# Fourier layer of a two-layer diffusion block: adding and subtracting mirrored tokens ahead of the input projection

## Chip, cores and metric

The kernel runs on one core of one Trainium2 chip. The metric is the device time of one execution in microseconds (us); lower is better.

## What is computed

Two layers run over 2048 latent tokens of 1024 channels in float32. Layer 0 is attention. Layer 1, which the change touches, mixes by a two-dimensional Fourier transform: over the positions, and over the 256 channels of each of four groups. Cut to what matters:

```python
def fourier_layer(x, shift, scale, gate, norm_g, w_in, w_out):
    h = modulate(x, norm_g, shift, scale)
    u, g = jnp.split(h @ w_in, 2, axis=-1)
    uf = u.reshape(b, n, F_GROUPS, F_GROUP_DIM).astype(jnp.float32)
    f = jnp.fft.fft2(uf, axes=(1, 3), norm="ortho").real.astype(x.dtype).reshape(b, n, F_WIDTH)
    return x + gate * ((f * jax.nn.silu(g)) @ w_out)
```

The real part of the transform of u needs, of every channel group, a cosine transform over the channels (even in the position's sign) and a sine transform (odd in it). So only sums of tokens n and N-n meet the cosine part, and only differences meet the sine part.

## The kernel before

Every float32 product is made of three matmuls in a rounded one-pass type: `split` (lines 43 to 51) writes an operand as a high and a low part, `mm3` (lines 54 to 57) multiplies high by high, high by low and low by high. The phases are 1 (input projection of layer 0), 2 (attention, in a hand-written order), 3a (its output projection, and the modulated norm of layer 1 written to DRAM as `h2`, lines 768 to 826), 3b (Fourier input projection), 3c (transform over positions, lines 972 to 1045) and 3d (output projection and final norm). Outside phase 2 a planner orders each engine's instructions by its own estimate of when they are ready; the chip then runs each engine's queue in that order.

At the start, `startup` (line 203) multiplies the left half of the layer's weights by the channel transform, so that 3b projects straight into transformed channels; 32 pieces of 128x256 are evacuated by ScalarE and stored to DRAM as `wur` by ScalarE's DMA queue (lines 236 and 237), cosine and sine columns of a group in one store.

The tokens lie in four blocks of 512: n, N/2-n, N/2+n and N-n. Phase 3b (line 941) runs twice, first over the blocks n and N-n, then over N/2-n and N/2+n. Each run goes through four sets of 512 columns: cosine (`ci` 0), sine (1), and two sets of the gate (2, 3). For each set `load_w4` loads and splits the weights into tiles `whi`, `wlo` of two rows of tiles each (five buffers), with GpSimd for the high and VectorE for the low part. For each block `load_h2` loads `h2` once, in eight pieces `hraw` of 128x512 (four buffers), and splits them into `ghi`, `glo`. Each of the four 128-token tiles of a block takes 24 matmuls of 512 columns for each set. Of sets 0 and 1 the first block's result is copied to `z`; the second's meets it on VectorE, which folds n with N-n (`fold_first`) and then N/2-n with N/2+n onto the first fold (`fold_second`), and ends with the operands EH, EL, OH, OL and the second ones E1, O1. Of the gate's sets the result goes through Silu and is stored as `g2`. `nyq` and N1, NH, NL carry the middle channel of each group; `quarter` carries the tokens N/4 and 3N/4, which have no partner.

All loads named here go through SP's DMA queue (`ld`), all stores through ScalarE's (`st`); each queue issues in order. SBUF is handed out from two sides, and pools that follow each other reuse the same bytes: a tile waits for the last reader of what lay there. Phase 3c loads its 12 tables `ch`, `cl`, `sh`, `sl` through GpSimd's queue, for three sets of positions (258, 256 and 512 columns), into bytes that phase 3b used; its matmuls are as in 3b, with 258, 256 and 512 columns.

Of the kernel before, what the change touches and what calls it, by code (L numbers as in the profile page):

```python
# [35 lines left out]
NDFT = 1026  # L36
TOKEN_GROUPS = (0, 3, 1, 2)     # blocks of tokens in the order that folding takes them

# input projection columns
# [47 lines left out]
def block_kernel(ctx: ExitStack, tc: tile.TileContext, a):  # L87
# [23 lines left out]
    wur_d = [dt_(f"wur{i}", [P, D]) for i in range(8)]  # L111
# [3 lines left out]
    # ---------------------------------------------------------------- constants  # L115
# [16 lines left out]
    # lambda on every partition, negated  # L132
# [12 lines left out]
    # bounded where the reference's norm is zero anyway; an infinite lambda still gives NaN  # L145
# [4 lines left out]
    # the score scale goes with the query gain (a power of two for the other heads)  # L150
# [30 lines left out]
    def rstd(ss, n, inv):  # L181
        """1 / sqrt(ss * inv + eps), one Newton step on the table's root."""
# [20 lines left out]
    def startup(pool, grp, pp, cb):  # L203
        """Modulations of layer 0, and W_u times the real channel transform for every group."""
        rc = pool.tile([P, 2, 256], F32, name="rc")
# [7 lines left out]
        for g in range(4):  # L213
            for b in range(2):
# [15 lines left out]
                for dt in range(4 * b, 4 * b + 4):  # L230
                    ps = pp.tile([P, 512], F32, name="wur", tag="mm", bufs=5)
                    for k in range(2):
                        T.matmul(ps[:, 0:256], u[k][:, (dt % 4) * P:(dt % 4 + 1) * P], rc[:, k, :],
                                 start=k == 0, stop=k == 1)
                    o = pool.tile([P, 256], F32, name="wuo", tag="wuo", bufs=4)
                    S.copy(o, ps[:, 0:256])
                    st(wur_d[dt].rearrange("p (s c) -> p s c", s=2)[:, :, g * P:(g + 1) * P],
                       o.rearrange("p (s c) -> p s c", s=2))
# [3 lines left out]
    # ------------------------------------------------- phase 1: input projection  # L242
    with ExitStack() as ph:
# [51 lines left out]
        def rope(src, cos, sin, nh, dim):  # L295
            """src * cos + swap(src) * sin, the halves of each axis swapped."""
# [28 lines left out]
        def put_T(src, dsts, t, stack=False):  # L325
# [4 lines left out]
            if stack:  # L330
                # rows of each half: 64 rounded, then 64 of what rounding left
# [12 lines left out]
        def evac(kind, ps, t, rp):  # L344
            """ps: 128 tokens x 512 columns of the projection; t: key tile."""
# [25 lines left out]
        # modulations of layer 1 and both gates, a tile at a time  # L371
# [61 lines left out]
    class Factors:  # L433
        """Of the differential heads' rows, s1 * o each, at the tokens of groups g0 to g1:
        1 / sqrt(mean(o^2) + eps), and zero where the reference's sum of squares leaves float32."""
# [4 lines left out]
        def steps(self, pool):  # L440
            """One instruction at a time."""
# [28 lines left out]
    # ------------------------------------------------------- phase 2: attention  # L470
    with ExitStack() as ph:
# [7 lines left out]
        KP = L // 3                                   # columns of a key or value piece  # L479
        QT = 256                                      # queries of a pair of tiles  # L480
# [3 lines left out]
        def load_split(pool, src, name, eng=(None, None)):  # L484
            """Thirds of a [128, L] scratch array as hi and lo."""
# [18 lines left out]
        def load_q(rows, tag, eng=(None, None)):  # L504
            """rows: DRAM row sets stacked on partitions."""
# [8 lines left out]
        class Task:  # L514
            """Scores of 128 queries against all keys, and exp(s - max) with its row sum."""
# [4 lines left out]
            def S(self, i):  # L520
                """Scores of segment i, which the task before has left."""
# [13 lines left out]
            def M(self, i):  # L535
                """Maximum of a segment."""
# [8 lines left out]
            def E(self, i):  # L545
                """exp of a segment."""
# [7 lines left out]
            def X(self):  # L554
                """Row sum; the first of a combination is ready with it."""
# [15 lines left out]
            def Z(self):  # L571
                """Subtracts the second probabilities, times lambda and in units of the first's sum."""
# [6 lines left out]
            def tail(self, op, i):  # L579
                """The same of the very last, in parts and on two engines."""  # L580
# [14 lines left out]
        class Pair:  # L595
            """o^T of 256 queries from two probability tiles."""
# [4 lines left out]
            def F(self):  # L601
                """Rows of a pair that is through."""
# [4 lines left out]
            def Q(self):  # L607
                """Their squares, and over the channels the sums of these."""
# [11 lines left out]
        class Item:  # L620
            """Two key tiles of a pair: transposes, split, V^T P^T."""
# [54 lines left out]
        def begin(n):  # L676
            """Pairs, tasks and items of a step: 256 queries of a head, and what they need."""
# [72 lines left out]
    def out_proj(pp, lp, us, wg, x, add):  # L750
        """x += gate * u^T w for the tokens i of x's four tiles; yields each i when done."""
# [16 lines left out]
    with ExitStack() as ph:  # L768
# [9 lines left out]
        def second_mod(x, t):  # L778
            """Modulated norm of x for layer 1, transposed."""
# [48 lines left out]
    # --------------------------- phase 3b: Fourier input projection, token folding  # L828
    with ExitStack() as ph:
        dp = ph.enter_context(ExitStack())  # L830
        sp = dp.enter_context(tc.tile_pool(name="eo", bufs=1, reuse_waits="tile"))
        # tokens n and N/2 - n folded onto n < N/4: sums (even positions) as hi and lo, and
        # differences (odd positions)
        EH, EL, OH, OL = [sp.tile([P, 4, 512], F32R, name=nm) for nm in ("EH", "EL", "OH", "OL")]
# [4 lines left out]
        with ExitStack() as pb:  # L839
# [54 lines left out]
            def fold_second(ci, j, z, ps):  # L894
                """Tokens N/2 - n (z) and N/2 + n (ps): the second fold."""
                if j == 0:
                    quarter(ci, ps)
# [312 lines left out]
```

## Time and profile before

| | |
|---|---|
| time, median of 3 runs | 2800.76 us (2798.21 to 2805.19) |
| span of the profiled execution, first to last instruction | 2799.0 us |
| mean granted clock of TensorE, share of full speed | 0.979 |
| TensorE busy with matmuls | 2675.6 us, 96% of the span |
| VectorE, ScalarE, GpSimd busy | 1762.1, 1395.5, 1201.1 us |
| phase 3b on TensorE | about 2193 to 2548 us |
| phase 3c on TensorE | about 2548 to 2598 us |

The profile gives no time of the profiled execution beyond its span; the span lies 1.8 us below the median of the runs and inside their range. Matmuls are pipelined: the profile gives one of 512 columns some 0.39 us, but the next one starts 0.23 us later, so what a matmul costs is read from the distance of starts. A line such as L55 to L57 is that of the helper `mm3`, so groups are told apart by their tiles; the moving operand stands first (`mm<-whi,ghi` has the weights moving over stationary tokens: sets 0 and 1; `mm<-ghi,whi` is the gate).

### The profile page before, as it was taken

How to read it: one execution, taken by the hardware profiler on the slowest of the kernel's cores; microseconds unless marked ns; L12 is line 12 of the kernel's file. 1: busy time of each engine (PE TensorE's matmuls, PEld its weight loads, DVE VectorE, ACT ScalarE, POOL GpSimd, SP SyncE). 2: the span in 40 equal slices, each digit the busy share in tenths (PEclk: the TensorE clock that was granted, in tenths of full speed). 3: DMA queues.
4: the chain of work that ended last, by engine and by line, in shares of the span. 5: the costliest groups of instructions: out<-in, count | busy, mean ns of one | idle time of the engine just before them, and what ended most of it. 6: DMA issues, size and time to landing. Idle time of an engine off the chain costs nothing.

```text
span 2799.0 us, 44286 instructions
## 1 busy us (share of the span) xinstructions
PE 2675.6 (96%) x15452; PEld 2322.7 (83%) x15452; DVE 1762.1 (63%) x3817; ACT 1395.5 (50%) x3700; POOL 1201.1 (43%) x1120
## 2 busy tenths in 40 slices
PE   4999998999989999999999999999899899999898
PEld 3788887887869999999989999998788688888687
DVE  7653635655248888888878888888663312322754
ACT  3631214312148888788878888888353302111312
POOL 3131421324157667766876777765322111011400
PEclk7999999999999999999999999999999999999999
DMA  9356354463410002000300011002683523128342
GB/s 325 114 140 181 93 164 160 108 188 97 147 66 20 18 20 71 18 20 20 97 23 20 20 46 31 20 19 76 215 273 132 176 75 133 48 76 226 119 153 91
DMA packets 217775, 282.51 MB, mean 101 GB/s; under 512 B 19184, under 2 KB 130496, under 8 KB 217552
## 3 DMA queue, kind: packets, MB, share of 16 engines
q1 hardware_dynamic: 115984, 197.84, 22.1%
q10 hardware_dynamic: 95232, 73.43, 8.4%
q0 software_dynamic: 6336, 8.41, 1.3%
q8 instruction: 123, 2.02, 0.3%
q14 instruction: 100, 0.82, 0.1%
HBM read 197.74 MB, written 81.83 MB: 100 GB/s over the span
## 4 chain that ended last, share of the span: by engine, by line
PE 70%; DVE 3%; POOL 1%; DMA 1%; issue 1%; ACT 1%; SPq 0%; DVEq 0%; ACTq 0%; POOLq 0%
PE s L531 16%; PE mm L57 9%; PE mm L55 9%; PE mm L56 9%; PE ptr L631 9%; PE pv L55 5%; PE pv L57 5%; PE pv L56 5%; DVE m L539 1%; PE tr L785 1%; POOL e L593 0%; PE s L615 0%; DMA u<-uy 0%; DVE tl L639 0%; PE pa L55 0%
## 5 line engine op out<-in xcount | busy, mean ns | idle before, releaser
L539 DVE TENSOR_REDUCE m<-s 128x1 f32<-128x512 f32 (+1 forms) x960 | 579.0, 632 | 174.0 <-PE s L531 169.1
L551 ACT ACTIVATE e<-s,nm 128x512 f32<-128x512 f32 (+1 forms) x960 | 614.2, 653 | 51.3 <-DVE nm L543 47.9
L635 ACT CAST th<-ptr 128x512 fp32r<-128x512 f32 x576 | 340.3, 591 | 145.6 <-PE ptr L631 130.6
L639 DVE TENSOR_TENSOR tl<-ptr,th 128x512 fp32r<-128x512 f32 x576 | 379.3, 681 | 38.3 <-ACT th L635 38.2
L57 PE MATMUL mm<-whi,glo 128*128 128x512 f32 x944 | 372.5, 396 | 3.9 <-DVE glo L51 3.9
L55 PE MATMUL mm<-whi,ghi 128*128 128x512 f32 x944 | 370.4, 396 | 1.8 <-DVE ghi L50 1.8
L56 PE MATMUL mm<-wlo,ghi 128*128 128x512 f32 x944 | 371.6, 395 | 0.0
L631 PE MATMUL ptr<-ident,e 128*128 128x128 f32 x2304 | 349.5, 274 | 20.2 <-DVE tl L639 11.4
L593 POOL TENSOR_TENSOR e<-e 128x768 f32<-128x768 f32 x189 | 342.7, 1844 | 0.0
L48 POOL TENSOR_SCALAR whi<-wraw 128x1024 fp32r<-128x1024 f32 x88 | 106.3, 1211 | 523.0 <-PE mm L56 200.3
L631 PEld LDWEIGHTS ptr<-ident,e 128*128 128x128 f32 x2304 | 271.9, 141 | 48.2 <-POOL e L593 7.2
L531 PE MATMUL s<-kB,qh 128*128 128x512 f32 (+1 forms) x768 | 285.0, 380 | 6.8 <-ACT e L551 6.8
L590 POOL TENSOR_SCALAR e<-e,rs 128x768 f32<-128x768 f32 x192 | 170.6, 912 | 220.2 <-DVE rs L566 220.2
L531 PE MATMUL s<-kB,ql 128*128 128x512 f32 (+1 forms) x768 | 252.0, 341 | 0.0
L51 DVE TENSOR_TENSOR wlo<-wraw,whi 128x1024 fp32r<-128x1024 f32 x88 | 114.1, 1299 | 181.8 <-POOL whi L48 181.7
L308 POOL TENSOR_TENSOR t<-qn,rope 128x256 f32<-128x256 f32 (+1 forms) x128 | 116.2, 929 | 252.2 <-issue 102.9
L57 PEld LDWEIGHTS mm<-whi,glo 128*128 128x128 f32 x944 | 178.2, 189 | 42.5 <-DVE glo L51 5.5
L55 PEld LDWEIGHTS mm<-whi,ghi 128*128 128x128 f32 x944 | 178.5, 189 | 39.4 <-issue 2.0
L56 PEld LDWEIGHTS mm<-wlo,ghi 128*128 128x128 f32 x944 | 178.3, 189 | 36.7
L551 ACT ACTIVATION_READ_ACCUMULATOR e<-s,nm 128x1 f32 x960 | 201.7, 210 | 0.0
L55 PE MATMUL mm<-ghi,whi 128*128 128x512 f32 x512 | 199.7, 391 | 0.0
L56 PE MATMUL mm<-glo,whi 128*128 128x512 f32 x512 | 197.9, 389 | 0.0
(280 smaller groups left out, 6164.2 us busy)
## 6 DMA issues: line engine op xcount, KB each, us to landing
wraw<-in_w_in SPq DMA_DIRECT2D x56, 512.0 KB, 3.9
aw<-in_adaT SPq DMA_DIRECT2D x64, 256.0 KB, 3.0
g<-sg ACTq DMA_DIRECT2D x64, 256.0 KB, 2.5
gl<-g SPq DMA_DIRECT2D x64, 256.0 KB, 5.8
kB<-kB SPq DMA_DIRECT2D x24, 384.0 KB, 3.8
awr<-in_adaT SPq DMA_DIRECT2D x32, 256.0 KB, 4.9
xt<-in_x SPq DMA_DIRECT2D x16, 512.0 KB, 4.4
ql<-qB SPq DMA_DIRECT2D x128, 64.0 KB, 2.2
```

Of the source, the lines that this page charges most:

```text
L55: nc.tensor.matmul(out, lh, rh, start=start, stop=False)
L56: nc.tensor.matmul(out, lh, rl, start=False, stop=False)
L57: nc.tensor.matmul(out, ll, rh, start=False, stop=stop)
L308: Q.tensor_tensor(out=o5[:, :, :, b, :], in0=s5[:, :, :, 1 - b, :], in1=sn[:, :, b, :].unsqueeze(1).to_broadcast([P, nh, 2, q]), op=ALU.mult)
L531: T.matmul(ps[:, c - o:c - o + cw], l, r[c // KP][:, k:k + cw], start=(j == 0), stop=(j == len(self.terms) - 1))
L539: V.tensor_reduce(out=self.m3[:, i:i + 1], in_=self.segs[i][:, 0:SEG[i][1]], axis=AX.X, op=ALU.max)
L551: S.activation(self.e[:, o:o + w], self.segs[i][:, 0:w], AF.Exp, bias=self.nm, accum_out=self.s3[:, i:i + 1])
L590: eng.tensor_scalar(out=self.e[:, sg], in0=self.e[:, sg], scalar1=by, scalar2=1.0, op0=ALU.mult, op1=ALU.mult)
L593: eng.tensor_tensor(out=onto[:, sg], in0=onto[:, sg], in1=self.e[:, sg], op=ALU.add)
L631: T.transpose(self.tr[:, k, i, :], self.p.es[i][:, kt * P:(kt + 1) * P], ident)
L635: S.copy(self.th, self.tr.rearrange("p k i q -> p k (i q)"))
L639: V.tensor_tensor(out=self.tl, in0=self.tr.rearrange("p k i q -> p k (i q)"), in1=self.th.bitcast(F32), op=ALU.subtract)
```

## The change

Mirrored blocks of `h2` are added or subtracted before the projection instead of after it. A fold (`load_fold`) loads the pieces of both blocks of a pair, adds or subtracts them on VectorE, sets the token without a partner with one or two GpSimd instructions on a single column, and splits the result. `project` sends sums through the cosine columns alone and differences through the sine columns alone. The gate's sets move into `gates`, which loads `h2` by itself. The order is now: gate of the first pair, sums and differences of the first pair, differences and sums of the second, gate of the second pair. The operands share one ring of 20 tiles (high and low part of one 128x512 piece each).

The middle channel gets a column of its own among the cosines, so that there are 4 x 129 = 516 of them, done as two matmuls of 258 columns; `wur` grows to 1028 columns and is stored by two DMAs for each piece instead of one. Token N/4 of the sums goes through a projection of its own, one row wide. Nothing else of phases 1 to 3a and 3d changes; 3c takes the middle channel from EH, EL.

```diff
-                    st(wur_d[dt].rearrange("p (s c) -> p s c", s=2)[:, :, g * P:(g + 1) * P],
-                       o.rearrange("p (s c) -> p s c", s=2))
+                    st(wur_d[dt][:, g * 129:(g + 1) * 129], o[:, 0:129])
+                    st(wur_d[dt][:, CW + g * P:CW + (g + 1) * P], o[:, 129:257])
...
+            def operand(src):
+                t = hp.tile([P, 2, G], F32R, name="hl", tag="hl", bufs=20)
+                split(nc, t[:, 0, :], t[:, 1, :], src, S)
+                return t[:, 0, :], t[:, 1, :]
+            def load_raw(g, kt):
+                raw = wk.tile([P, G], F32, name="hraw", tag="hraw", bufs=4)
+                ld(raw, h2_d[:, kt, g * G:(g + 1) * G])
+                return raw
+            def load_fold(half, op):
+                out = []
+                for kt in range(KT):
+                    a_, b_ = [load_raw(g, kt) for g in TOKEN_GROUPS[2 * half:2 * half + 2]]
+                    e = wk.tile([P, G], F32, name="hf", tag="hf", bufs=2)
+                    V.tensor_tensor(out=e, in0=a_, in1=b_, op=op)
+                    if op is ALU.add or half == 0:
+                        Q.tensor_copy(e[:, 0:1], a_[:, 0:1])
+                        if half == 0 and op is ALU.add:
+                            Q.tensor_copy(h34[:, kt:kt + 1], b_[:, 0:1])
+                    else:
+                        Q.tensor_tensor(out=e[:, 0:1], in0=b_[:, 0:1], in1=h34[:, kt:kt + 1], op=ALU.subtract)
+                        Q.tensor_tensor(out=h4[:, kt:kt + 1], in0=b_[:, 0:1], in1=h34[:, kt:kt + 1], op=ALU.add)
+                    out.append(operand(e))
+                return out
...
+            def project(ci, half, hs):
+                whi, wlo = load_w4(ci)
+                cols = ((0, 258), (258, 258)) if ci == 0 else ((0, 512),)
+                one, hi_, lo_ = ((E1, EH, EL), (O1, OH, OL))[ci]
+                for j in range(4):
+                    ms = slice(j * P, (j + 1) * P)
+                    for c, w in cols:
+                        ps = pp.tile([P, 512], F32, name="mm", tag="mm", bufs=5)
+                        cs = slice(c, c + w)
+                        for kt in range(KT):
+                            mm3(nc, ps[:, 0:w], hs[kt][0][:, ms], hs[kt][1][:, ms], whi[kt][:, cs], wlo[kt][:, cs],
+                                kt == 0, kt == KT - 1)
+                        e1 = one[:, j, cs]
+                        if half == 0:
+                            S.copy(e1, ps[:, 0:w])
+                            continue
...
+                        V.tensor_tensor(out=e, in0=e1, in1=ps[:, 0:w], op=(ALU.add, ALU.subtract)[ci])
+                        V.tensor_tensor(out=e1, in0=e1, in1=ps[:, 0:w], op=(ALU.subtract, ALU.add)[ci])
+                        split(nc, hi_[:, j, cs], lo_[:, j, cs], e, S)
+                if half == 1 and ci == 0:
+                    for c, w in cols:
+                        for kt in range(KT):
+                            mm3(nc, ps[0:1, 0:w], h4h[:, kt:kt + 1], h4l[:, kt:kt + 1],
+                                whi[kt][:, c:c + w], wlo[kt][:, c:c + w], kt == 0, kt == KT - 1)
...
+            gates(0)
+            project(0, 0, load_fold(0, ALU.add))
+            project(1, 0, load_fold(0, ALU.subtract))
+            odd_ = load_fold(1, ALU.subtract)
+            split(nc, h4h, h4l, h4)
+            project(1, 1, odd_)
+            project(0, 1, load_fold(1, ALU.add))
+            gates(1)
```

## Rows read from the trace of the kernel before

**Rows 1.** Page: span, and each engine's busy time, share and instructions.
```profile
span 2799.0 us, 44286 instructions
PE 2675.6 (96%) x15452; PEld 2322.7 (83%) x15452; DVE 1762.1 (63%) x3817; ACT 1395.5 (50%) x3700; POOL 1201.1 (43%) x1120
```
**Rows 2.** Page: chain of work that ended last, share by engine.
```profile
PE 70%; DVE 3%; POOL 1%; DMA 1%; issue 1%; ACT 1%; SPq 0%; DVEq 0%; ACTq 0%; POOLq 0%
```
**Rows 3.** Windows, phase 3b, its early loads, early 3c; its first row names columns.
```profile
core 0: us, PE busy (x) PEld busy (x) DVE busy (x) ACT busy (x) POOL busy (x), PEclk, DMA share, GB/s
2193.00:2549.00 356.00, 356.00 (x1556) 291.55 (x1555) 92.66 (x152) 54.02 (x94) 44.50 (x39) 0.99 0.32 100
2206.00:2214.00 8.00, 8.00 (x37) 6.63 (x36) 4.79 (x8) 5.19 (x9) 0.00 (x0) 1.00 0.77 254
2548.00:2574.00 26.00, 26.00 (x219) 25.01 (x218) 15.58 (x43) 4.86 (x9) 2.22 (x3) 1.00 0.84 246
```
**Rows 4.** Groups by form, phase 3b, TensorE: one set-0/1 group, one gate group.
```profile
L57 PE MATMUL mm<-whi,glo 128*128 128x512 f32 x256 | 100.7, 395 | 0.0
L55 PE MATMUL mm<-ghi,whi 128*128 128x512 f32 x256 | 100.0, 392 | 0.0
```
**Rows 5.** Timeline of TensorE, 512 columns, first and last of 33 consecutive starts.
```profile
2204.64 0.39 PE L57 MATMUL mm<-whi,glo 128*128 128x512 f32 x1
...
2211.90 0.39 PE L56 MATMUL mm<-wlo,ghi 128*128 128x512 f32 x1
```
**Rows 6.** Timeline of TensorE, 258 and 256 columns: start, and first start behind 216.
```profile
2548.25 0.28 PE L55 MATMUL pn<-ch,NH 128*4 128x258 f32 x1
...
2573.89 0.40 PE L55 MATMUL pn<-ch,NH 128*4 128x512 f32 x1
```
**Rows 7.** Groups by form, 2550 to 2574 us: weight loads of those matmuls.
```profile
L56 PEld LDWEIGHTS pb<-sl,OH 128*128 128x128 f32 x32 | 6.0, 188 | 0.0
```
**Rows 8.** DMA view, 2206 to 2214 us: loads, count, KB each, us to landing.
```profile
hraw<-h SPq DMA_DIRECT2D x8, 256.0 KB, 3.5
```
**Rows 9.** Waits of SP's queue, phase 3b: us in total, times, longest.
```profile
SPq L867 <- DVE wlo L51: 112.8, 14, 34.8
```
**Rows 10.** Groups by form, phase 3b, VectorE, ScalarE and GpSimd: busy, mean ns.
```profile
L51 DVE TENSOR_TENSOR wlo<-wraw,whi 128x1024 fp32r<-128x1024 f32 x30 | 37.5, 1251 | 106.5 <-POOL whi L48 106.5
L51 DVE TENSOR_TENSOR glo<-hraw,ghi 128x512 fp32r<-128x512 f32 x30 | 20.5, 716 | 24.5 <-ACT ghi L46 24.3
L915 DVE TENSOR_TENSOR e<-E,e 128x512 f32<-128x512 f32 x4 | 2.8, 692 | 0.1
L46 ACT CAST ghi<-hraw 128x512 fp32r<-128x512 f32 x27 | 16.1, 621 | 19.2 <-DMA hraw<-h 18.5 <-ACT h L789 0.4
L48 POOL TENSOR_SCALAR whi<-wraw 128x1024 fp32r<-128x1024 f32 x30 | 38.4, 1283 | 283.6 <-PE mm L56 100.4 <-DVE e L915 67.2 <-PE mm L57 67.0
```
**Rows 11.** Groups by form, 2598 to 2645 us, GpSimd busy 34 of 47 us.
```profile
L1077 DVE TENSOR_TENSOR u<-FL,gl 128x512 f32<-128x512 f32 x6 | 8.1, 1348 | 0.1
```
**Rows 12.** Instructions of one line, start-up: ns min/median/max, first and last start.
```profile
L237 ACTq DMA_DIRECT2D wur<-wuo x32: 520/521/654, 17.9 to 93.5; - x32
```
**Rows 13.** Timeline of GpSimd, phase 3c's table loads: first of each stretch, and last.
```profile
2527.06 0.96 POOL L997 DMA_DIRECT2D ch<-in_dft_ch  x1 [19.98 <-ACT sg L959]
...
2554.92 0.74 POOL L997 DMA_DIRECT2D cl<-in_dft_cl  x1 [19.23 <-DVE eL L51]
...
2556.38 0.76 POOL L997 DMA_DIRECT2D sl<-in_dft_sl  x1
```
**Rows 14.** DMA view, 2525 to 2575 us: last table load of two sets, us to landing.
```profile
sl<-in_dft_sl POOLq DMA_DIRECT2D x1, 1024.0 KB, 15.1
sl<-in_dft_sl POOLq DMA_DIRECT2D x1, 512.0 KB, 18.3
```
**Rows 15.** Timeline of TensorE, end of phase 3a.
```profile
2191.79 1.94 PE L785 MATMUL tr<-ident,xn 128*128 128x128 f32 x8 [11.74 <-DVE xn L201]
```

More of the change, by code (lines that the diff above doesn't have):

```diff
@@ L110, in block_kernel @@
     x1_d = [dt_(f"x1{i}", [P, D]) for i in range(NT)]
-    wur_d = [dt_(f"wur{i}", [P, D]) for i in range(8)]
+    wur_d = [dt_(f"wur{i}", [P, CW + 512]) for i in range(8)]
     s1_d = [dt_(f"s1r{g}", [4 * NG, P]) for g in range(NG)]
@@ L841, in block_kernel @@
             wp = pb.enter_context(tc.tile_pool(name="p4w", bufs=2, reuse_waits="tile", side="right"))
[L842 to L843 removed]
+            hp = pb.enter_context(tc.tile_pool(name="p4g", bufs=1, reuse_waits="tile", side="right"))
             wk = pb.enter_context(tc.tile_pool(name="p4k", bufs=3, reuse_waits="tile"))
[L845 removed]
@@ L846, in block_kernel @@
-            fold = pb.enter_context(tc.tile_pool(name="p4f", bufs=1, reuse_waits="tile"))
+            zp = pb.enter_context(tc.tile_pool(name="p4z", bufs=1, reuse_waits="tile"))
+            h34 = zp.tile([P, KT], F32, name="h34")
+            h4 = zp.tile([P, KT], F32, name="h4")
+            h4h, h4l = [zp.tile([P, KT], F32R, name=nm) for nm in ("h4h", "h4l")]
+            def operand(src):
+                t = hp.tile([P, 2, G], F32R, name="hl", tag="hl", bufs=20)
+                split(nc, t[:, 0, :], t[:, 1, :], src, S)
+                return t[:, 0, :], t[:, 1, :]
@@ L848, in load_h2 @@
+            def load_raw(g, kt):
+                raw = wk.tile([P, G], F32, name="hraw", tag="hraw", bufs=4)
+                ld(raw, h2_d[:, kt, g * G:(g + 1) * G])
+                return raw
             def load_h2(g):
-                grp = g0p if g < 2 else g1p
-                hi = grp.tile([P, KT, G], F32R, name="ghi", tag="ghi")
-                lo = grp.tile([P, KT, G], F32R, name="glo", tag="glo")
+                return [operand(load_raw(g, kt)) for kt in range(KT)]
+            def load_fold(half, op):
+                out = []
@@ L852, in load_h2 @@
                 for kt in range(KT):
-                    raw = wk.tile([P, G], F32, name="hraw", tag="hraw", bufs=4)
-                    ld(raw, h2_d[:, kt, g * G:(g + 1) * G])
-                    split(nc, hi[:, kt, :], lo[:, kt, :], raw, S)
-                return hi, lo
+                    a_, b_ = [load_raw(g, kt) for g in TOKEN_GROUPS[2 * half:2 * half + 2]]
+                    e = wk.tile([P, G], F32, name="hf", tag="hf", bufs=2)
+                    V.tensor_tensor(out=e, in0=a_, in1=b_, op=op)
@@ L941, in block_kernel, with quarter @@
-            for half in range(2):
+            def quarter(row, dst, n, w, blocks):
+                tr = pp.tile([P, 512], F32, name="qtr", tag="qtr", bufs=2)
+                for i, (c, cw) in enumerate(blocks):
+                    T.matmul(tr[0:cw, i:i + 1], row[0:1, c:c + cw], ones[0:1, 0:1], start=True, stop=True)
+                V.tensor_copy(dst, tr[0:n, 0:w])
+            def project(ci, half, hs):
[14 more added lines that the diff above has]
+                            continue
+                        if ci == 1 and j == 0:
+                            row = zp.tile([1, CW + 4], F32, name="row", tag="row")[:, 0:512]
+                            V.tensor_copy(row, ps[0:1, :])
+                            quarter(row, O4, P, 4, [(g * P, P) for g in range(4)])
+                        e = wk.tile([P, 512], F32, name="e", tag="ee", bufs=2)[:, 0:w]
+                        V.tensor_tensor(out=e, in0=e1, in1=ps[:, 0:w], op=(ALU.add, ALU.subtract)[ci])
+                        V.tensor_tensor(out=e1, in0=e1, in1=ps[:, 0:w], op=(ALU.subtract, ALU.add)[ci])
+                        split(nc, hi_[:, j, cs], lo_[:, j, cs], e, S)
+                if half == 1 and ci == 0:
+                    row = zp.tile([1, CW + 4], F32, name="row", tag="row")
+                    for c, w in cols:
+                        ps = pp.tile([P, 512], F32, name="mm", tag="mm", bufs=5)
+                        for kt in range(KT):
+                            mm3(nc, ps[0:1, 0:w], h4h[:, kt:kt + 1], h4l[:, kt:kt + 1],
+                                whi[kt][:, c:c + w], wlo[kt][:, c:c + w], kt == 0, kt == KT - 1)
+                        V.tensor_copy(row[:, c:c + w], ps[0:1, 0:w])
+                    V.tensor_copy(row[:, CW:CW + 4], row[:, 128:CW:129])
+                    quarter(row, E4[:, 0:4], P, 4, [(g * 129, P) for g in range(4)])
+                    quarter(row, E4[0:4, 4:5], 4, 1, [(CW, 4)])
@@ L942, in block_kernel, with gates @@
+            def gates(half):
                 groups = TOKEN_GROUPS[2 * half:2 * half + 2]
                 gh = {}
-                for ci in range(4):
+                for ci in (2, 3):
                     whi, wlo = load_w4(ci)
-                    zt = {}
                     for g in groups:
@@ L1155, in _rmat @@
     c, s = np.cos(ang) / 16.0, np.sin(ang) / 16.0
-    s[:, 0] = np.where(d[:, 0] % 2 == 0, 1.0, -1.0) / 16.0
-    return np.concatenate([c, s], 1).astype(np.float32)
+    s[:, 0] = 0.0
+    middle = np.where(d % 2 == 0, 1.0, -1.0) / 16.0
+    return np.concatenate([c, middle, s], 1).astype(np.float32)
 def _frow_perm():
```

117 lines of the change are left out of this document (23 added, 94 removed).

## Prediction, made before the changed kernel was run

> **What bounds the kernel now.** I read the page first: TensorE is busy for 2675.6 of 2799.0 us, the next engine for 63% [rows 1], and TensorE holds 70% of the chain that ended last [rows 2]. That is an average over phases, so the phase of the change is read by itself. In the window of 3b, 2193 to 2549 us, TensorE is busy for all 356 us at a granted clock of 0.99, while VectorE works 93, ScalarE 54 and GpSimd 45 us, and the DMA engines are busy for 0.32 of the time [rows 3]. So a matmul that disappears there shortens the kernel by the distance of its start to the next one, as long as the operands of what remains arrive in time. Whether they do is the question of this change: it multiplies a phase's loading and vector work and squeezes the middle of it.
>
> **TensorE's part.** Sets 0 and 1 have three groups of 256 matmuls of 512 columns, 768 in all; the gate has as many [rows 4]. Their starts are (2211.90 - 2204.64)/32 = 0.2269 us apart [rows 5]; 1536 of them make 348.5 us, which is the window but for its slow first microseconds. The change leaves 16 row tiles instead of 32 (four calls of `project`, four tiles each). The two sine calls have 2 x 4 x 24 = 192 matmuls of 512 columns, 43.6 us. The two cosine calls have 384 of 258 columns. Phase 3c has this shape: 216 matmuls of 258 and 256 columns between 2548.25 and 2573.89 us, 0.1187 us each [rows 6], with a full weight load ahead of nearly each one. So 384 cost 45.6 us. The one-row projection of token N/4 adds 48 matmuls of 258 columns with one stationary column; the nearest row has four such columns and starts at the same pace [rows 6], so 5.7 us. Removed 174.3, added 94.9: a gain of 79.4 us, all on the path. The tiny matmuls of `quarter` replace as many transposes and are taken at nothing.
>
> **Supply of the four calls.** A fold loads 16 pieces of 256 KB, a weight set 8 more: 24 for a call that lasts 22 or 23 us on TensorE (28 for the last). Before, a pair's pieces were loaded once for 174 us of matmuls. Eight `hraw` loads in the window from 2206 to 2214 us ran at 254 GB/s, with the engines at 0.77 [rows 3, 8]: 1.03 us a load, 24.8 us a call. Against that stands a lead. The ring has 20 tiles; the gate of the first pair holds 16, four are free from the start, and eight come free when its first block is done with, a quarter of the gate (22 us) before its end. So 12 of the 32 folded tiles can be there when the first call starts. The other 20, with three weight sets, are 40 + 24 = 64 loads, 16.8 MB or 66 us at that rate, and TensorE gives about 66 us before it needs the last of them. Nothing is left over, but nothing is short. VectorE needs 8 x (0.692 + 0.716) for a fold and 4 x 1.251 for the weights, 16.3 us a call, and 8.3 (four tiles by three operations at 0.692) to some 10 us more in the two calls of the second pair [rows 10]: 26 us against 22 to 28, again with the lead to draw on. ScalarE's casts (8 x 0.621) and GpSimd's (4 x 1.283) are short. The trace has no GpSimd instruction on a single column; 48 are added, in a chain VectorE, GpSimd, ScalarE, VectorE for each piece. At VectorE's price of a full piece, 0.692, they would be 33 us over four calls, under GpSimd's idle time; what they delay is the piece behind them, and four raw buffers, two pairs, cover one such delay. For the whole supply the lower bound is 0 (a gain is excluded, since TensorE has no idle time here [rows 3]). The upper: 24 loads one behind the other with no overlap of weights and pieces cost 24.8 us plus a piece's 0.692 + 0.621 + 0.716 for each call, some 27 us; four calls 108 against the 89 us of their matmuls, 19 us late. I take 5, nearer the lower end, because in the stretch of heaviest loading the engines were at 0.77 and TensorE did not stop [rows 3].
>
> What is queued behind what: SP's queue issues in order, and weight loads sit in it for up to 34.8 us until a buffer is split [rows 9]. Before, nothing behind them was urgent. Now the next fold's pieces may stand there; the planner decides, and five banks of PSUM let it start other tiles on the weights that are there. GpSimd's casts of weights wait for TensorE's last use in the same way [rows 10], and the single-column instructions stand in that queue too.
>
> On the same units, the Trainium skill (page "SBUF — State Buffer", section "SBUF: two separate sides") says that VectorE with two SBUF inputs and GpSimd share a port pair that one of them locks for a whole instruction while the other stands still. The trace agrees where both are busy: a VectorE product of 0.69 us takes 1.348 on average while GpSimd is busy 34 of 47 us [rows 10, 11]. By that rule GpSimd's 5.1 us of casts a call would be added to VectorE's 26, 31 against 22 to 28, some 12 us over the two late calls instead of the 5 of my sum: 2738 us.
>
> **The two joins and the start.** Start-up: 32 more stores at 0.521 us of ScalarE's queue [rows 12], 16.7 us at the worst if all lay on the path, 0 if ScalarE's idle time takes them; a gain is excluded, since only work is added. ScalarE waits there for products of other engines much of the time, so 1. Join of 3a and 3b: TensorE waits 11.74 us for the last norm [rows 15]; the gate's loads are as many as the old first set's, but their tiles now lie on other bytes of 3a. If a filled gap is one end, -11.7, and eight loads late by 1.03 the other, +8, I take 1, since the gap ends with the norm and not with a load. End of 3b: by the sizes of the pools, the last three operand tiles of the closing gate lie where the tables of 3c's second set go (right side: 49.5 KB of weights, then the ring; the tables lie below 48 KB of results and constants). Before, all eight tables of the first two sets left GpSimd from 2527 us on and only three of the third set after the gate, from 2554.92 us, the last landing 15.1 us behind its issue at 2556.38 [rows 13, 14], 2571.5, with 2574 as the time of need. Now the second and third set, 6.3 MB, start with the gate's end. The second set is needed 12.7 us later; four tables landed within 18.3 us of issue where they queued behind four others [rows 14]. At 246 GB/s [rows 3] 6.3 MB take 25.6 us, and the third set is needed 25.6 us after the gate's end. Between 0 and 10 us; 3, by the row of the rate. A gain is excluded, as the tables were in time before.
>
> **Sum.** 79.4 - 5 - 3 - 1 - 1 = 69.4 us. The span of 2799.0 becomes 2729.6; the profiled execution's time beyond the span is not given, and the median lies 1.8 above the span, so 2731 us.
>
> **Rivals.** First, supply paces the calls: the upper bound of 19 instead of 5, and 0 to 15 more where VectorE's queue is late too: 2745 to 2760. For it: loads, vector work and TensorE's time of a call are within some us of each other. Against it: the lead of 12 tiles. Second, the other side: the planner queues each fold's loads behind weight loads that wait for the call before, so that supply and matmuls alternate. Four calls by 24 loads of 1.03 us are 99 us in place of the 5: 2825, slower. It decides from where three quarters of the loading (74 of 99 us) stands between the calls. For it speaks the 34.8 us wait at the head of SP's queue [rows 9]; against it, that the ring has room half a call ahead and that the planner sees such waits. Third, the change does not save what it counts: the 258-column matmuls are paced by their weight loads of 0.188 us [rows 7], 432 x (0.188 - 0.119) = 30 us lost, 2761. Against it: the same pairs run at 0.1187 in 3c [rows 6, 7].
>
> **How the numbers follow.** Forecast 0.66; supply 0.23; alternation 0.06; weight loads 0.05. Range 2714 to 2762: below, all costs at nothing (2721) and a part of the gap of 11.7 us filled; above, the first and third rival, which leaves out the second. A measurement here tells 0.3%, 8.4 us, from no change. Faster by more: all but the second rival and a little of the first, 0.93; within, 0.02; slower 0.05.
>
> **What would show it.** In the profile after: `mm` groups of 258 columns with starts 0.12 us apart, and 192 of 512 columns with moving weights where there were 768; the stretch from the first `mm` matmul to the first `pn` at some 277 to 290 us instead of 355. If idle time of TensorE stands inside it, released by VectorE's low parts or by `hraw` loads, the first rival is at work; if it stands at the four starts of calls, some 20 us each, the second. Idle time at the second `pn` with a table as releaser confirms the join. The prediction is wrong if the phase is as short as said and the time is not.

## The result

The changed kernel takes 2762.97 us (median of four runs, 2761.71 to 2767.78) against 2801.61 for the kernel before beside it (2798.21 to 2805.19): a ratio of 0.9867, 95% interval 0.9852 to 0.9882. It is faster by 38.6 us, where some 70 were forecast (2731), and lies 1 us above the range of 2714 to 2762. The page of after, beside [rows 1]:

```profile
span 2760.7 us, 44341 instructions
PE 2609.4 (95%) x15317; PEld 2269.3 (82%) x15317; DVE 1790.1 (65%) x3834; ACT 1412.1 (51%) x3730; POOL 1218.4 (44%) x1168
```

TensorE's busy time fell by 66.2 us and the span by 38.3, so other time came in. Each trace is divided at the same seven events (first or last start in a tile's group): the first `mm` matmul, the first maximum `m` of attention, the last `mm<-w0h,ul` of 3a, the first `mm` of 3b, the first `pn`, the last `pb`, the end. The stages, in us, for every kernel below:

| kernel | to first `mm` | projections of phase 1 | attention, 3a | join | 3b | 3c | 3d | span |
|---|---|---|---|---|---|---|---|---|
| before | 90.0 | 705.4 | 1382.0 | 16.0 | 354.9 | 49.9 | 200.8 | 2799.0 |
| after | 98.7 | 717.2 | 1377.8 | 25.0 | 285.9 | 56.1 | 200.0 | 2760.7 |
| e1_two_stores | 98.4 | 719.2 | 1381.7 | 15.9 | 354.9 | 50.0 | 200.7 | 2820.8 |
| e2_one_store | 91.0 | 706.2 | 1383.4 | 25.2 | 288.3 | 52.7 | 200.8 | 2747.6 |
| e5_sixteen_stores | 88.7 | 721.9 | 1383.6 | 24.5 | 289.5 | 52.5 | 200.8 | 2761.5 |
| s1_eight_buffers | 94.9 | 713.5 | 1380.4 | 25.7 | 286.6 | 52.6 | 200.4 | 2754.1 |
| s2_three_buffers | 107.4 | 707.2 | 1382.8 | 24.5 | 286.0 | 55.7 | 200.8 | 2764.4 |
| s3_blocks | 90.2 | 717.1 | 1382.9 | 25.4 | 287.7 | 53.2 | 200.3 | 2756.8 |
| j3_load_order | 99.3 | 720.5 | 1377.9 | 15.0 | 289.9 | 56.0 | 201.0 | 2759.6 |
| j6_order_and_place | 97.7 | 718.2 | 1379.4 | 14.6 | 287.6 | 58.1 | 200.9 | 2756.5 |
| p1_keep_sine | 98.6 | 719.1 | 1380.7 | 24.4 | 285.7 | 55.4 | 200.6 | 2764.5 |
| t1_table_place | 98.5 | 719.6 | 1380.4 | 25.3 | 287.5 | 50.6 | 205.4 | 2767.3 |
| c1_all | 91.8 | 706.3 | 1380.1 | 15.0 | 287.6 | 50.7 | 205.0 | 2736.5 |
| c4_tables_inputs | 92.5 | 706.7 | 1382.6 | 15.2 | 287.1 | 50.6 | 211.8 | 2746.5 |
| c3_sixteen_stores | 89.2 | 707.9 | 1381.6 | 15.5 | 288.5 | 50.7 | 211.7 | 2745.1 |
| c5_queue_order | 92.1 | 708.1 | 1381.6 | 15.0 | 289.3 | 50.7 | 201.9 | 2738.7 |

From before to after: +8.7 +11.8 -4.2 +9.0 -69.0 +6.2 -0.8 = -38.3. The stage of the change gave 69.0. The start with the projections behind it (20.5), the join (9.0) and 3c (6.2) cost 35.7, where the prediction put 5 for the start, the join and the tables together; attention and 3d gave 5.0 back.

In 3b the matmuls are as counted (192 of 512 columns with moving weights, 384 and 48 of 258). Timeline of TensorE in after, a cosine call, first and last of 52 consecutive starts, (2331.96 - 2325.84)/51 = 0.120 us apart [rows 6]:

```profile
2325.84 0.28 PE L57 MATMUL mm<-wlo,hl 128*128 128x258 f32 x1
...
2331.96 0.28 PE L57 MATMUL mm<-wlo,hl 128*128 128x258 f32 x1
```

Waits of TensorE from 2219 to 2505 us (total, times, longest; the first row started before the stretch and belongs to the join):

```profile
PE mm L56 <- ACT hl L47: 11.7, 1, 11.7
PE mm L56 <- POOL whi L49: 3.2, 3, 2.2
PE mm L57 <- DVE wlo L52: 0.5, 2, 0.4
```

The start-up's stores, which answer to [rows 12]: 64 issues where there were 32.

```profile
L238 ACTq DMA_DIRECT2D wur<-wuo x32: 326/326/527, 18.4 to 103.6; - x32
L239 ACTq DMA_DIRECT2D wur<-wuo x32: 326/447/571, 19.7 to 104.1; - x32
```

The projections of phase 1 lose most of theirs in one place. Window from 138 to 178 us, the row of before and then that of after (columns as in [rows 3]): TensorE starts 142 instructions instead of 189, and the granted clock is 0.87 on average: from 161.6 to 171.9 us, behind a stop, it is 1.2 instead of 2.4 GHz. The longest wait there is the third row, that of a matmul for a copy by ScalarE.

```profile
138.00:178.00 40.00, 40.00 (x189) 32.36 (x188) 30.64 (x82) 16.60 (x63) 16.32 (x18) 1.00 0.55 154
```

```profile
138.00:178.00 40.00, 31.82 (x142) 25.24 (x141) 26.82 (x86) 19.28 (x71) 9.25 (x11) 0.87 0.44 131
```

```profile
165.87 0.80 PE L56 MATMUL mm<-whi,ghi 128*128 128x512 f32 x1 [5.31 <-ACT vv L357]
```

At the join of 3a and 3b, SP's queue in after (a merged row: start, duration, count). Twelve weight loads, some waiting for bytes and buffers, stand ahead of the first piece of `h2`; before, that piece was issued at 2174 us:

```profile
2164.09 49.62 SPq L896 DMA_DIRECT2D wraw<-in_wg  x12
2213.76 1.86 SPq L860 DMA_DIRECT2D hraw<-h  x4
```

At 3c, GpSimd's table loads, which answer to [rows 13]. The last eight start with the gate's end at 2505 us, and the last one to land stops TensorE:

```profile
2505.28 0.74 POOL L1000 DMA_DIRECT2D ch<-in_dft_ch  x1 [23.88 <-PE mm L58]
...
2510.40 0.81 POOL L1000 DMA_DIRECT2D sl<-in_dft_sl  x1
```

```profile
2540.09 0.50 PE L57 MATMUL pb<-sl,oH 128*128 128x512 f32 x1 [3.18 <-DMA sl<-in_dft_sl]
```

### The profile page after: what moved, and what is told of

The parts are those of the page before. It is cut to its first block, busy times and chain, and to the rows that moved or that the text cites. A ratio compares the mean times of both kernels' runs of the same rounds, so it can differ in the third digit from the quotient of the medians.

```text
span 2760.7 us, 44341 instructions
## 1 busy us (share of the span) xinstructions
PE 2609.4 (95%) x15317; PEld 2269.3 (82%) x15317; DVE 1790.1 (65%) x3834; ACT 1412.1 (51%) x3730; POOL 1218.4 (44%) x1168
## 4 chain that ended last, share of the span: by engine, by line
PE 64%; DMA 4%; DVE 3%; POOL 2%; issue 1%; ACT 1%; SPq 0%; ACTq 0%; DVEq 0%; POOLq 0%
PE s L532 17%; PE ptr L632 9%; PE mm L56 8%; PE mm L58 8%; PE mm L57 8%; PE pv L56 5%; PE pv L58 5%; PE pv L57 5%; DMA hraw<-h 1%; DMA sl<-in_dft_sl 1%; POOL e L594 1%; PE tr L786 0%; DVE m L540 0%; PE s L616 0%; DVE wlo L52 0%
## 5 line engine op out<-in xcount | busy, mean ns | idle before, releaser
L56 PE MATMUL mm<-whi,ghi 128*128 128x512 f32 x688 | 271.6, 398 | 7.2 <-ACT vv L357 5.3
L58 PE MATMUL mm<-whi,glo 128*128 128x512 f32 x688 | 272.6, 397 | 2.9 <-DVE glo L52 2.9
L57 PE MATMUL mm<-wlo,ghi 128*128 128x512 f32 x688 | 271.4, 396 | 0.0
L49 POOL TENSOR_SCALAR whi<-wraw 128x1024 fp32r<-128x1024 f32 (+1 forms) x88 | 105.2, 1198 | 350.9 <-PE mm L57 141.2
L52 DVE TENSOR_TENSOR wlo<-wraw,whi 128x1024 fp32r<-128x1024 f32 (+1 forms) x88 | 114.3, 1302 | 152.6 <-POOL whi L49 152.5
L591 POOL TENSOR_SCALAR e<-e,c 128x768 f32<-128x768 f32 x189 | 168.7, 910 | 23.4 <-DVE c L575 15.5
L56 PE MATMUL pv<-th,vAh 128*128 128x256 f32 x576 | 170.3, 296 | 0.2 <-ACT oT L605 0.2
L56 PE MATMUL pv<-th,vBh 128*128 128x256 f32 x576 | 165.3, 287 | 0.0
L57 PE MATMUL pv<-tl,vAh 128*128 128x256 f32 x576 | 161.1, 280 | 0.0
L58 PE MATMUL pv<-th,vAl 128*128 128x256 f32 x576 | 160.9, 279 | 0.0
```

The lines of the kernel that those rows point to most:

```text
L56: nc.tensor.matmul(out, lh, rh, start=start, stop=False)
L57: nc.tensor.matmul(out, lh, rl, start=False, stop=False)
L58: nc.tensor.matmul(out, ll, rh, start=False, stop=stop)
L591: eng.tensor_scalar(out=self.e[:, sg], in0=self.e[:, sg], scalar1=by, scalar2=1.0, op0=ALU.mult, op1=ALU.mult)
```

## The experiments

Each is told by its stage in the table; "after" is the changed kernel.

### The start: number of stores, or order of the plan

**e1_two_stores**, on the kernel before:

```diff
-    st(wur_d[dt].rearrange("p (s c) -> p s c", s=2)[:, :, g * P:(g + 1) * P], o.rearrange("p (s c) -> p s c", s=2))
+    st(wur_d[dt][:, g * P:(g + 1) * P], o[:, 0:128])
+    st(wur_d[dt][:, 512 + g * P:512 + (g + 1) * P], o[:, 128:256])
```

> The kernel before with one edit: each of the 32 combined pieces of the first stage is stored with two issues of 128x128 in place of one of 128x2x128, so that 64 issues stand on the ACT queue as in the kernel after; matrices, matmuls and bytes are those of before. Theory A (the second issue per piece is what made the first stage of the kernel after 20 us longer: it holds ACT, whose sums feed the next pieces): the first `mm` of the first projection starts at 97 to 101 us instead of 90.0, the first attention output `m` at 810 to 816 instead of 795.4, and the whole run is 12 to 20 us slower than before. Rival B (the 258-column combine and the runs of 516 bytes cost it, not the count): nothing moves by more than 3 us. Rival C (the issues cost only their own time, 32 more of about 0.33 to 0.45 us on an engine with idle time): 0 to 4 us.

2822.05 us, ratio 1.0067 (1.0052 to 1.0082): 19.8 us slower, with nothing of the Fourier change in it. First `mm` 98.4, first `m` 817.6. Theory A's numbers came, but for the first `m`, 1.6 us later than it said; those of B and C did not. Two of ScalarE's waits up to 100 us; in before, no row of stores stands there, and the one behind GpSimd is longer (last row), so not all of the 15.0 us is new:

```profile
ACT awr L229 <- DMA wur<-wuo: 15.0, 4, 5.4
ACT awr L229 <- POOL awr L228: 14.6, 7, 3.1
```

```profile
ACT awr L229 <- POOL awr L228: 22.7, 9, 4.8
```

What such an issue waits for can be read from the semaphores in the traces. The transfers of SP's and of ScalarE's queue report their landing by the same eight semaphores, and an issue may have to stand until the transfer that last used its semaphore has landed. In after, 19 of the 64 store issues start within 0.1 us of such a landing, and ScalarE stands still for 14.8 us before them (e1: 18 and 14.2); in before it is 8 of 32, and 7.3 us. No run changes the number of semaphores, so how much of the later first `mm` this makes is not shown.

**e2_one_store**, on after: the sine columns padded to 129, so that one store takes both parts.

```diff
-    wur_d = [dt_(f"wur{i}", [P, CW + 512]) for i in range(8)]
+    wur_d = [dt_(f"wur{i}", [P, 2 * CW]) for i in range(8)]
...
-    st(wur_d[dt][:, g * 129:(g + 1) * 129], o[:, 0:129])
-    st(wur_d[dt][:, CW + g * P:CW + (g + 1) * P], o[:, 129:257])
+    st(wur_d[dt].rearrange("p (s c) -> p s c", s=2)[:, :, g * 129:(g + 1) * 129], o.rearrange("p (s c) -> p s c", s=2))
```

> The kernel after with the sine columns padded to 129 for each quarter, so that one issue of 128x2x129 stores each combined piece as in the kernel before (32 issues in place of 64); the second projection reads the 4x128 columns out of 4x129. Theory A (the count of issues): the 16 to 20 us of the first stage come back: first `mm` at 89 to 92 us, first attention output at 795 to 799 instead of 815.9, total 2743 to 2750. Rival B (the odd widths: 516-byte runs and a 258-column combine): the first stage stays where it was in the kernel after, 98.7 and 815.9, total 2760 to 2766. Rival C (the padded moving operand slows the second projection): its matmuls start more than 0.2269 us apart and the stage of the projections grows by over 5 us.

2750.02 us, ratio 0.9806 (0.9789 to 0.9822). First `mm` 91.0, first `m` 797.2: 18.7 us back. Some of it went again in attention (1383.4 against 1377.8). Rival B falls: the 258-column combine and the odd runs are in this kernel too. Rival C falls too: 3b grew by 2.4 us, where it said over 5.

**e5_sixteen_stores**, on e2: two pieces in one `wuo` of 516 columns (three buffers), one store of 128x4x129.

> The kernel with one store per combined piece (the run e2_one_store), now with two pieces per store: 16 issues of 128x4x129 in place of 32 of 128x2x129. Theory A carried on (each issue on the ACT queue of the first stage holds ACT while the transfers are full): the first `mm` of the first projection comes at 84 to 89 us instead of 91.0, the first attention output at 785 to 794 instead of 797.2, total 2738 to 2746. Rival J (32 issues are below the point from which they decide; POOL's products and the loads set the pace there): first `mm` at 90 to 93, first attention output 795 to 799, total within 3 us of that run's 2750.

2762.08 us. The first `mm` did come earlier, 88.7. But the projections behind it took 721.9 instead of 706.2, so the first `m` stood at 810.6: fewer issues, and the loss of after was back. So the number of issues can't be the cause of the loss behind the first `mm`. The planned order of TensorE's instructions tells more (X is a transpose of the norm, T one of the rotated keys, mm a matmul; number in a row):

```
before, e2:  X24 mm24 X8 mm19 X4 mm1 X4 mm30 X8 mm10 X4 mm10 X4 mm37 X8 mm2 X4 mm20 X4 mm29 X8 T2 mm23 T2 mm5 T2 ...
after, e1:   X24 mm59 X12 mm13 X4 mm48 X16 mm48 X16 mm48 X8 T8 mm21 T4 mm24 T4 ...
e5:          X16 mm12 X4 mm12 X4 mm32 X8 mm10 X4 mm6 X4 mm47 X12 mm1 X4 mm48 X16 mm48 X8 T8 mm21 T4 ...
```

The planner lays out all of phase 1 from when it believes each tile to be ready; another number of issues at the start tips it into long blocks. At X8 T8 TensorE has no matmuls to put between: two transposes wait some 1 us each for ScalarE's `h`, and the matmul behind them 5.3 us for its copy to `vv`, which is the window shown above. Three kernels change the order without the stores, by the number of `wuo` buffers alone.

**s1_eight_buffers**: after, `bufs=8`. 64 stores, short runs (X8 mm22 X8 mm23 ... T2 mm21 T2).

> The kernel after with eight `wuo` buffers in place of four, and nothing else: still two stores for each combined piece, 64 issues, but the planner then lays the projections of the first phase out as in the kernel before (transposes in eights and twos between short runs of matmuls) and not in blocks of 48 matmuls and 16 transposes. Theory K (of the 20.5 us, the 8.7 to the first `mm` are the issues, and the 11.8 behind it are the planner's other order, whatever the issues cost): first `mm` at 94 to 100 us, from there to the first attention output 704 to 709 us instead of 717.2, total 8 to 14 us below the kernel after. Rival A (the 64 issues cost it all): 716 to 721 us from the first `mm` to the first attention output, total within 4 us of the kernel after.

2756.81 us, ratio 0.9838. First `mm` 94.9, projections 713.5: between the theories. In the window of 138 to 178 us TensorE starts 186 instructions, so the hole of after is closed; another, of 2.5 us behind VectorE with the lower clock after it, opened at 177 us.

**s3_blocks**: e2 with `bufs=5`. 32 stores, long blocks.

> The run e2_one_store (32 stores, one for each combined piece) with five `wuo` buffers instead of four: the planner then lays the first projections out in blocks of 48 matmuls and 16 transposes, as in the kernel after. Theory K (that order costs the 12 us behind the first `mm`, whatever the number of stores): first `mm` at 89 to 93 us, from there to the first attention output 715 to 723 us instead of 706.2, total 9 to 16 us above that run's 2750. Rival A (the stores' number costs it): 704 to 708 us, total within 3 us of 2750.

2761.61 us; first `mm` 90.2, projections 717.1. As theory K said, the hole is there with 32 stores. Its window, 145 starts and clock 0.87:

```profile
138.00:178.00 40.00, 32.31 (x145) 25.86 (x144) 26.61 (x93) 17.46 (x70) 10.57 (x13) 0.87 0.53 153
```

**s2_three_buffers**: after with `bufs=3`. 64 stores, short runs in twos.

> The kernel after with three `wuo` buffers instead of four: 64 stores, and the planner lays the first projections out in short runs with transposes in twos, as in the kernel before. Theory K: 704 to 709 us from the first `mm` to the first attention output instead of 717.2; the first `mm` itself may come later, at 98 to 104 us, for want of a buffer. Theory N (both: the order, and the stores still behind it on ACT's queue, as the run with eight buffers gave with 713.5): 711 to 715 us. Rival A: 716 to 722 us.

2762.80 us: projections 707.2, as K said, though the first `mm` came at 107.4, later than expected, for want of a buffer:

```profile
138.00:178.00 40.00, 40.00 (x192) 32.97 (x191) 28.69 (x94) 18.52 (x71) 9.23 (x12) 1.00 0.52 144
```

So the 20.5 us are two things. To the first `mm`, the stores on ScalarE's queue: with four buffers 89.2 us for 16 issues (c3), 90.0 to 92.5 for 32, 97.7 to 99.3 for 64; with 64 the buffers count too, 107.4 for three and 94.9 for eight. Behind it, the order: 717 to 722 in long blocks with 16, 32 or 64 stores, 705 to 708 in short runs (713.5 in one case).

### The join

**j3_load_order**: the first eight pieces of `h2` are queued in turns with the first weights.

```diff
+    if half == 0 and ci == 2:
+        gh[groups[0]] = load_h2(groups[0])
+        behind = dict(at)              # the eight load instructions
...
+    with tc.issue_after(behind[kt]):
+        ld(raw[:, k, :], a["wg2"][kt * P:(kt + 1) * P, (ci - 2) * 512:(ci - 1) * 512])
```

> The kernel after with the order of the sync queue changed at the start of the stage of the projections, and nothing else: the first eight `hraw` loads stand in turns with the first eight weight loads instead of behind twelve of them. Theory D (the 9 us at that join are the place of the `hraw` loads in the queue): the pause between the last transposes of the output stage and the first `mm` of the gates falls from 25.9 us to 15 to 18, total 8 to 11 us less. Rival E (the memory: `hraw` lies on tiles of the output stage that come free last, and the weight loads behind it now wait for them too): the pause stays at 24 to 30 us, total within 4 us of the kernel after.

2762.06 us, ratio 0.9855. The join fell from 25.0 to 15.0 us, so D holds for the pause, but the total did not move: 4.0 went in 3b, which now starts with its weights short, and the profiled run was 3.9 later at the first `m`. SP's queue now, first rows, and a wait of TensorE in 3b that was 3.2 us in after:

```profile
2197.87 6.59 SPq L862 DMA_DIRECT2D hraw<-h  x4
2206.65 6.16 SPq L897 DMA_DIRECT2D wraw<-in_wg  x3
```

```profile
PE mm L56 <- POOL whi L49: 5.4, 7, 1.5
```

**j6_order_and_place**: the same, with `hraw`, the raw weights and the output tiles in pools of their own on the right side, over bytes that 3a frees early.

> As the run before it, and `hraw`, the raw weights and the first tiles of the `hl` ring laid on memory that the output stage frees early (its input tiles and a gap that it doesn't use) instead of on its last `xn2` and gate tiles. Theory D (order alone decides): no more than 3 us better than with the order alone. Rival E (place decides): the pause at the join falls from 25.9 us to 5 to 14, and the total is 12 to 20 us below the kernel after.

2761.11 us, ratio 0.985. Join 14.6: the place adds nothing there (E falls, its 5 to 14 was not reached): it is the order alone. 3c gives some back, since this layout puts the ring over the tables: `ch` of the first set left at 2455.51, the next table 42 us later, with the gate's end, and TensorE stood 5.2 us for it.

```profile
2498.23 0.75 POOL L1012 DMA_DIRECT2D cl<-in_dft_cl  x1 [41.75 <-PE mm L58]
```

### Supply inside 3b

**p1_keep_sine**, on after:

```diff
-    whi, wlo = load_w4(ci)
+    whi, wlo = w4 or load_w4(ci)
...
-    project(1, 1, odd_)
+    project(1, 1, odd_, sine_)      # the weights that project(1, 0) returned
```

> The kernel after with the sine weights of the second projection call kept for the third, so that one of the eight sets of weights of that stage (8 loads, 4 POOL casts, 4 DVE lows) isn't loaded. Theory H (of the 286 us of the stage some 15 are lost to supply, a good part of it where a call waits for the `whi` of its own weights): the waits for `whi` at that one boundary go, the stage takes 282 to 285 us, total 1 to 4 us below. Rival I (the losses stand elsewhere, at the start of the stage and at half clock behind it): the stage takes 285.5 to 287, total within 1 us.

2761.87 us; 3b 285.7 instead of 285.9. Rival I: one weight set fewer, of eight, buys nothing.

### The tables, and what lies behind them

**t1_table_place**, on after: the first table set over `hraw` and the sums, the other two over ring tiles of the gate's first block; one odd split (`oL`) to the right side; and the table loads queued behind the last cast of weights.

> The kernel after with another place for the tables of the stage of the cosine and sine transforms and for the four odd splits beside them, and nothing else: the first set lies on the bytes of the raw tiles and sums, the second and third on ring tiles of the next to last gate group, which are free some 22 us before the gates end; in the kernel after the second and third set lie on tiles of the last group and are issued only at the gates' end. Theory F (that stage takes 56.1 us instead of 49.9 because its last table lands 29.6 us after an issue that waits for the gates' last matmul): all twelve issues stand before the first `pn`, TensorE waits for no table, the stage takes 49 to 51.5 us, total 4 to 7 us below the kernel after. Rival G (the 6 us are the 516-byte and 512-byte products themselves or the splits of the odd parts, not the tables): the issues come earlier and the stage still takes 54 to 57 us.

3c 50.6 us, as F said, with no wait for a table. But 2766.88 us: 3d grew from 200.0 to 205.4. A `gl` load on bytes that 3c's `pa` matmuls still read stood at the head of SP's queue until 2559.6 us, 2.4 ahead of 3c's end, and the first weights of 3d left 1.1 us ahead of that stage, in after 29 us. So its first matmul waits 6.5 us for a weight, where after's waits 4.0, and the stage spends 30.9 us at the lower clock instead of 13.9:

```profile
2559.55 0.80 SPq L1086 DMA_DIRECT2D gl<-g  x2
```

```profile
PE mm L56 <- ACT w1h L47: 6.5, 1, 6.5
```

**c1_all**: e2, j3, t1 and p1 together.

> One store per piece, the sync queue's order at the join, the place of the tables and the kept sine weights together, on the kernel after. If the causes are separate, their parts add up: first stage -13 to -20, join -10, projections -2 to +3, tables -5 to -6: total 2728 to 2742 us. If they are not (what is gained at the join is given back to the tables or to the supply), no more than the first edit's gain stays: 2744 to 2751 us.

2740.38 us, ratio 0.9788 (0.9772 to 0.9805). Stage by stage the parts add up: 91.8 and 706.3 as in e2, 15.0 as in j3, 50.7 and 205.0 as in t1.

**c4_tables_inputs**: c1 with the largest table set lowest, `oL` over the first set, and 3d's residual tiles `xr` swapped with the factors `gl`.

> The run c1_all with the places changed once more: there the transform stage kept its 50.7 us, but the last stage took 205.0 instead of 200 to 201, its first loads standing behind one whose bytes the second table set held to the end. Here the largest set and the fourth odd split lie where that stage loads late. Theory L (the queue behind that one load): the last stage takes 199 to 202 us, the transform stage stays at 50 to 52, total 2733 to 2738. Rival M (the last stage's first inputs are late for another reason, the transfers of tables among them): it stays at 204 to 206, total 2739 to 2743.

2747.00 us: 3d grew further, to 211.8, outside both theories. SP's queue shows why (some rows): theory L had the mechanism, as c5 will show, and my edit put the wrong tile at the head. By the sizes of the pools the first `xr` now lay on the last table of the third, largest set (not of the second, as the expectation for c5 has it), and stood at the head until 3c's last `pb`, with the first weights and factors of 3d behind it:

```profile
2510.00 1.75 SPq L1107 DMA_DIRECT2D gl<-g  x4
2535.14 0.80 SPq L1123 DMA_DIRECT2D xr<-x  x2
2536.46 2.14 SPq L742 DMA_DIRECT2D wr<-in_w_fout  x4
```

**c3_sixteen_stores**: c4 with e5's 16 stores and four `wuo` buffers, planned in short runs.

> The run above with 16 stores in the first stage instead of 32, and four `wuo` buffers, with which the planner lays the projections out in short runs. Theory K: first `mm` at 87 to 90 us instead of 91 to 92, and 704 to 709 us from there to the first attention output (e5_sixteen_stores, in long blocks: 721.9), total 2729 to 2736, 2 to 5 us below the run above. Rival A: 718 to 723 us, total 2744 to 2750.

2747.55 us. First `mm` 89.2, projections 707.9 where e5 with three buffers had 721.9: K. The total missed what was expected, through 3d's 211.7 and 1.4 more in 3b.

**c5_queue_order**: c4 with the first `xr` loads queued behind those of `fing`, `gy` and the fourth `gl`.

```diff
+    with ExitStack() as late:
+        for r in early if g == 0 else ():     # loads of fing, gy and the fourth gl
+            late.enter_context(tc.issue_after(r))
         ld(x, x1_d[4 * g + i])
```

> The run c4_tables_inputs, where the last stage took 211.8 us: its first load of the residual stood at the head of the sync queue from 2511.8 to 2535.1, to the end of the transform stage, on bytes of the second table set, with all others behind it. Here that load is queued behind the first weights, gates and factors, and nothing else is changed. Theory L (the queue behind that one load): the last stage takes 199 to 202 us, total 2730 to 2737. Rival M: 209 to 213 us, total 2744 to 2750.

2739.77 us, ratio 0.9767 (0.9752 to 0.9781). 3d is back at 201.9, with no tile moved. The first weights now leave 22 us sooner:

```profile
2514.33 2.50 SPq L742 DMA_DIRECT2D wr<-in_w_fout  x4
```

The total missed the expected 2737 by 3 us, of which 3b, with 289.3, took some 2; the kernel before, measured beside it, was 3.5 us slower than beside after. It and c1, level within their runs, beat after by 23 us and before by 61 to 65.

## Why the prediction went wrong where it did

- **TensorE's part, 79.4: right.** 258-column matmuls start 0.120 us apart, and the third rival (weight loads) is out. The stretch from the first `mm` to the first `pn` was forecast at 277 to 290 us and took 285.9.
- **Supply, 5: near, in its bounds.** 3b lost 79.4 - 69.0 = 10.4, and not all of it is supply. The distances between starts of matmuls, less 0.2269 us for 512 columns and 0.1187 for 258, leave 16.8 us in after's 3b and 6.3 in before's. Of the 10.4 between them, TensorE's stops are 4.5 (most of them behind GpSimd's casts), the lower clock 1.8, the tiny matmuls of `quarter`, taken at nothing, 1.4, and slower steps at full clock 2.7. Before and after, 512 columns start some 0.227 or 0.233 us apart, and after has more of the latter; why is open. p1 shows that a weight set fewer does not return the 10.4. By the port rule of the Trainium skill (page "SBUF — State Buffer", section "SBUF: two separate sides") the cost would have been some 12; but TensorE waited only 0.5 us for VectorE, so the runs don't show that price.
- **First rival.** It named 2745 to 2760, close to the time, for the wrong reason: of the 41.1 us of costs (10.4 + 20.5 + 9.0 + 6.2 - 4.2 - 0.8), supply took at most 6.3, the lower clock included. That the time lies only 1 us above the range, whose top this rival and the third set, is luck. The second rival did not come.
- **Start-up, 1 (0 to 16.7): the step that failed.** Measured +20.5 us. I priced 32 more issues by their own 0.52 us and let ScalarE's idle time take them. But an issue can also stand and wait for an earlier transfer, and 64 of them put the first `mm` 8.7 us later (e1 and e2 show that it is the issues). And I left out what lies behind: the planner re-planned a phase in which the change edits no line, 11.8 us. The bound was no bound, since it counted only the added instructions' own time. Attention gave 4.2 back, which no run explains.
- **Join, 1 (-11.7 to 8): outside its bound.** Measured +9.0. I counted eight loads and which bytes they lie on; what decided was the order in which SP's queue held them (j3: -10.0). The reason given, "the gap ends with the norm and not with a load", no longer held, since a load was late next.
- **Tables, 3 (0 to 10): right in place and kind.** Measured 6.2, with the wait at a table of the third set and not of the second (3.18 us, then some at the lower clock). Kernels that leave this stage alone took 52.5 to 56.1, so part of it moves with the landing of transfers; t1's 50.6 shows the rest.
- **Range.** It left out a stage that no edit touches. The sign and the 0.93 for faster were right.

## What to carry to other kernels

Where a planner orders the queues, count an added instruction twice: once for its own time, and once for the plan of everything behind it, which may be laid out anew; compare the planned order of phases that no edit touches before crediting a gain. Time won by freeing bytes or moving a load is only kept if the next load at the head of an in-order queue is ready: follow that queue to the next stage, as at the join, the tables and the last stage here.

## What the runs showed of the hardware

- A store's issue can cost more than its own duration. In after's start-up (DMA engines busy for 0.95 of the time from 16 to 62 us) the 64 issues show 0.33 and 0.45 us in the medians of their two lines, but ScalarE stood still for 14.8 us until earlier transfers on the same semaphores had landed.
- 258-column matmuls with a full weight load of 0.19 us each ran 0.120 us apart in 3b, where 3c gave 0.1187.
- A copy of a single column takes GpSimd 0.186 us in the median of 24, 0.41 on average and 1.07 at the most. The 48 single-column instructions took 17.5 us, where I had put 33 at the price of a full piece, 0.692.
